# Issuing the value products of two attention units together, in a two-layer hybrid transformer kernel

## The chip, the cores and the metric

The kernel runs on one core of a Trainium2 chip. The metric is the device time of one execution in microseconds; the median over runs is compared. A core has a matrix engine (TensorE, PE in the profile, with its weight loads as PEld), a vector engine (DVE), an activation engine (ACT), GpSimd (POOL) and a queue that issues transfers (SP).

## The reference

Two transformer layers over 512 positions of 1024 channels, one batch. In each layer the input is normalised and modulated by vectors worked out from `c`, and one projection gives the inputs of three kinds of attention with heads of 64 channels: four heads that attend to selected keys (A), four stick-breaking heads (B), eight heads with a window of 128 and sinks (C). Their outputs are normalised per head, projected by `w_o` and added; a gated feed-forward of width 2816 follows.

```python
# A: a top-256 mask from an index score, softmax over the selected keys
_, sel = lax.top_k(score, n_sel)
p = jax.nn.softmax(s, axis=-1)
out = jnp.einsum('bhqk,bqkd->bqhd', p.astype(vs.dtype), vs)
# B: weights from a reversed cumulative sum of log_sigmoid
a = jnp.where(strict, jnp.exp(jax.nn.log_sigmoid(z) + log_between), 0.0)
out = jnp.einsum('bhqs,bshd->bqhd', a.astype(v.dtype), v)
# C: a band of 128 keys, one sink for each head
p = e / (jnp.sum(e, axis=-1, keepdims=True) + jnp.exp(sink - m))
out = jnp.einsum('bkgqs,bskd->bqkgd', p.astype(vn.dtype), vn)
```

The last line of each kind is the value product: weights times values.

## The kernel before

Positions are cut into four tiles of 128. Everything large is a matmul of three terms on split operands (a high and a low part each): projections, `w_o`, gate, up and down. The attention work is woven into this stream.

The order of PE's instructions is fixed while the program is built, by a planner, the class `Weaver` (L62). It keeps a clock `now` that advances by an assumed duration of each PE instruction (L277: a matmul with a tile position counts as `PVNS` = 80 ns), and a list of tasks written as generators. A task that yields a number is resumed when the clock has gone on by that many nanoseconds; one that yields a condition waits for it. The numbers come from two tables, `LAT` (L53) for layer 0 and `LAT2` (L54) for layer 1. They stand for the time that other engines need between two PE steps: `z` and `zp` from the stick-breaking scores to the cumulative product, `cum` from there to the value product, `C` and `A` from a unit's scores to its transposes, `pT` from the transposes to the value product, `fin` from the last product of an output bank to the transposes of the normalised output, `evac` until an output bank is free. The main stream of projection matmuls runs when no task is due. On the chip the engines run in that order and wait for each other by semaphores.

PSUM banks are few: three for scores (tag `z`), one for transposes (`t`), one for outputs (`o`, NO = 1 at L41). The output bank has one owner at a time (`own`, L120).

A value product is `pv` (L660): two matmuls, one for each half of 64 columns of the transposed weights, with a tile position; each half takes 64 of the array's columns. Three places use it.

- `pairB` (L1031): one generator for each pair of stick-breaking heads and layer; three groups of key blocks (3 and 2; 1; 0). In each group come the scores of both heads, softplus on ACT and DVE, the cumulative products, an exponential on ACT into a tile `at` for each head (four such buffers), and then, with a yield for each head (L1089 to L1100), the value products: 12 or 16 matmuls a head.
- `unitC` (L1200): four units for each tile of positions, two heads each. Two units share an output bank (`a["bank", t, hf]`, L1189). A unit makes its scores, the mask and maximum on DVE, the exponential on ACT, transposes into the `t` bank, a copy of it on ACT into a tile `pT` (two buffers, L1242), and after `pT` nanoseconds its value products: 8 matmuls in the first tile, 16 in the others. The second unit of a bank goes on to `finish_o` (L741), which copies and normalises.
- `unitA` (L1302): four units for each tile, one head each, all four in one output bank; 4, 8, 12 or 16 matmuls.

While C and A run, the main stream has the `w_o` products of the heads that are ready (L1376 to L1415).

Of the kernel before, what the change touches and what calls it, by code (L numbers as in the profile page):

```python
# [15 lines left out]
P = 128  # L16
L = 512
D = 1024
NT = L // P
# [30 lines left out]
MODRATE = 1.36  # L50
RESTN = 3
WB, WC, WA, WI = 1, 4, 4, 2
LAT = dict(sq00=1978, sq10=1972, sq01=1520, sq11=3460, rs00=2100, rs01=2833, rs10=1750, rs11=1150, zi=7704, ev=2194, oT2=2213, rope=18712, score=58, z=3680, cum=682, zp=830, C=2868, A=4170, pT=1011, fin=6768, oT=3509, cons=9020, kc=9275, mod=1094, sq=1869, rs=1526, u=2835, evac=699)  # L53
LAT2 = dict(zi=4392, ev=667, oT2=3700, rope=11698, score=286, z=2932, cum=702, zp=700, C=5010, A=848, pT=1144, fin=7203, oT=2208, cons=11900, kc=8549, evac=798)  # L54
PROXY = lambda e: e
LAB = ["?"]
EXPSET = "natural_log_exp_and_others"
# [157 lines left out]
def kernel(ctx, tc, x, c, lns, w_mod, b_mod, w_nat, w_qk, gains, sinks, g_out,  # L215
# [3 lines left out]
    wv = Weaver()  # L219
# [593 lines left out]
    def attention(l):  # L813
        lat = LATS[l]
# [216 lines left out]
        def pairB(pr):  # L1031

            qT, kT = a["qbT"][pr], a["kbT"][pr]
            acc = [None, None]
            key = ("B", l, pr)
            ob = None
            for grp in ((3, 2), (1,), (0,)):
                yield wv.take(["zz", "z"])
                yield "z"
                wv.give("zz")  # L1040
                a["Bz"] += grp == (0,)
                with lab("B"):
                    zbs = [bank("z") for _ in range(2)]
                    lay = []
                    o0 = 0
                    for j in grp:
                        w = (NT - j) * P
                        lay.append((j, o0, w))
                        o0 += w
                    for j, a0, w in lay:  # L1050
                        for i, zb in enumerate(zbs):
                            hp = slice(i * 64, i * 64 + 64)
                            T.matmul(zb[:, a0:a0 + w], kT[hp, j * P:(j + 1) * P], qT[hp, j * P:], start=(a0 == 0),
                                     stop=False, skip_group_check=True)
                    sps = []
                    for zb in zbs:
                        for j, a0, w in lay:
                            T.matmul(zb[:, a0:a0 + P], identb, bmaskb, start=False, stop=True, skip_group_check=True)
                        e = slot("e")
                        S.activation(e[:, :o0], zb[:, :o0], AF.Abs)  # L1060
                        act(e[:, :o0], e[:, :o0], AF.Exp, scale=-1.0)
                        act(e[:, :o0], e[:, :o0], AF.Ln, bias=1.0)
                        sp = slot("sp")
                        V.scalar_tensor_tensor(sp[:, :o0], zb[:, :o0], 0.0, e[:, :o0], op0=OP.max, op1=OP.add)
                        sps.append(sp)
                ats = []
                for i, (zb, sp) in enumerate(zip(zbs, sps)):
                    yield lat["zp" if i else "z"]
                    with lab("B"):
                        for j, a0, w in lay:  # L1070
                            T.matmul(zb[:, a0:a0 + w], ltri, sp[:, a0:a0 + w], start=False, stop=(j == NT - 1),
                                     skip_group_check=True)
                            if j == 2:
                                T.matmul(zb[:, a0 + P:a0 + w], nones, sp[:, :P], start=False, stop=True,
                                         skip_group_check=True)
                            elif acc[i] is not None:
                                T.matmul(zb[:, a0 + P:a0 + w], nones, acc[i], start=False, stop=True,
                                         skip_group_check=True)
                        at = slot("at")
                        act(at[:, :o0], zb[:, :o0], AF.Exp)  # L1080
                        ats.append(at)
                        if len(grp) == 2:
                            G.tensor_add(sp[:, 2 * P:3 * P], sp[:, 2 * P:3 * P], sp[:, :P])
                            acc[i] = sp[:, P:3 * P]
                        elif grp[0]:
                            G.tensor_add(sp[:, P:3 * P], sp[:, P:3 * P], acc[i])
                            acc[i] = sp[:, :3 * P]
                    wv.give("z", lat["cum"])
                for i, at in enumerate(ats):  # L1089
                    yield lat["cum"] if i else lat["cum"] / 2, wv.own(key)  # L1090
                    with lab("B"):
                        first = ob is None
                        if first:
                            ob = bank("o")
                        obv = ob.rearrange("p (t h d) -> p t h d", t=NT, h=2)
                        for j, a0, w in lay:
                            for t in range(j, NT):
                                pv(obv[:, t, i, :], at[:, a0 + (t - j) * P:a0 + (t - j + 1) * P],
                                   a["vb"][j][:, (2 * pr + i) * 64:(2 * pr + i + 1) * 64], first, j == 0)
                                first = False  # L1100
            with lab("B"):
                onB = slot("wk", (P, NT, 2, 64))
                finish_o(ob, 8, None, "ob", onB.rearrange("p t h d -> p (t h d)"))
            wv.later(lat["evac"], lambda: wv.owners.discard(key))
            wv.add(outB(pr, onB))
            a["B"] += 1
# [67 lines left out]
        def cons_qc(hf):  # L1174
            def cons(t, pb):
                with lab("C"):
                    v = rms_of(pb[:, :256], 4, "cv")
                    nat = slot("nat")
                    V.tensor_mul(hd(nat[:, :256], 4), hd(pb[:, :256], 4), bc(gn[:, l, 2], 4))
                    r = rsqrt(v, 4, "cr", EPS, G)  # L1180
                    G.tensor_scalar(a["rc"][:, t, 4 * hf:4 * hf + 4], r, 0.125, None, op0=OP.mult)
                    rope_apply(hd(nat[:, :256], 4), hd(nat[:, :256], 4), 4, t)
                    q = stacked(nat[:, :256], 4)
                yield lat["cons"], "w"
                with lab("C"):
                    a["qcT"][t][hf] = slot("hid")
                    heads_t(a["qcT"][t][hf], q, 4, lat)
                wv.give("nat", 200)
                a["bank", t, hf] = {"n": 0, "ob": None}  # L1189
                yield lat["ev"]  # L1190
                for i in range(2):
                    wv.add(unitC(t, 2 * hf + i), "C", WC)
            return cons
# [6 lines left out]
        def unitC(t, i):  # L1200
# [34 lines left out]
            with lab("C"):  # L1235
# [4 lines left out]
                                    p2[:, hh * 256 + j * P:hh * 256 + (j + 1) * P], ident)  # L1240
                pT = slot("pT")
                S.copy(pT[:, :2 * n], tb[:, :2 * n])  # L1242
            yield lat["pT"], lambda: a["B"] == 2
            wv.give("t")
            with lab("C"):
                if B["ob"] is None:
                    B["ob"] = bank("o")
                for hh in range(2):
                    for j in range(nb_):
                        pv(B["ob"][:, loc[hh] * 64:(loc[hh] + 1) * 64],  # L1250
                           pT[:, (hh * nb_ + j) * P:(hh * nb_ + j + 1) * P],
                           a["vc"][k0 // P + j][:, g * 64:(g + 1) * 64], j == 0, j == nb_ - 1)
                B["n"] += 1
                if B["n"] == 2:
                    es = small(4, "ces")
                    V.tensor_sub(es, B["nb"], nsk[:, l, 4 * g:4 * g + 4])
                    act(es, es, AF.Exp)
# [16 lines left out]
        def cons_a(t, pb):  # L1274
# [20 lines left out]
            wv.give("nat", 200)  # L1295
            yield lat["ev"]
            a["ka"] += 1
            a["A", t] = {"n": 0, "ob": None}
            for h in range(4):
                wv.add(unitA(t, h), "A", WA)  # L1300

        def unitA(t, h):  # L1302
# [22 lines left out]
            with lab("A"):  # L1325
# [2 lines left out]
                    T.transpose(tb[:, j * P:(j + 1) * P], p[:, j * P:(j + 1) * P], ident)  # L1328
                pT = slot("pT")
                S.copy(pT[:, :n], tb[:, :n])  # L1330
            yield (lat["pT"], wv.take(["on"])) if B["n"] == 3 else lat["pT"]
            wv.give("t")
            with lab("A"):
                if B["ob"] is None:
                    B["ob"] = bank("o")
                for j in range(t + 1):
                    pv(B["ob"][:, h * 64:(h + 1) * 64], pT[:, j * P:(j + 1) * P], a["va"][j], j == 0, j == t)
                B["n"] += 1
                if B["n"] == 4:
                    on = slot("on")  # L1340
                    finish_o(B["ob"][:, :256], 4, B["den"], "oa", on[:, :256])
                    wv.later(lat["evac"], lambda: wv.owners.discard(key))
                    wv.add(out_t(0, 2, on, t, "outA"))
# [271 lines left out]
```

## Time and profile before

| what | us |
|---|---|
| three runs, median (lowest, highest) | 1293.27 (1291.34, 1295.54) |
| profiled execution | 1292.21 |
| its span, first to last instruction | 1290.4 |
| PE busy | 1246.3 (97%) |
| DVE busy | 803.1 (62%) |
| ACT busy | 551.4 (43%) |
| POOL busy | 143.8 (11%) |

A busy time is the union of the engine's instruction rows. A matmul's row lasts from its start to the end of its results, so rows of one stream overlap; the distance from start to start tells what one costs. Layer 0's attention with value products runs from about 107 to 271 us of the span, layer 1's from about 741 to 894.

### The profile page before, as it was taken

The page shows a single profiled execution, that of the slowest core. Times are in us where ns is not written, and L with a number is a line of the kernel's source. Part 1 is how long each engine was busy: PE and PEld are TensorE (multiplying, and loading weights), DVE is VectorE, ACT ScalarE, POOL GpSimd, SP SyncE. Part 2 cuts the span into 40 slices and gives each one's busy share as a digit, 9 for nine tenths or more (in the row PEclk, how much of TensorE's full clock was granted, in tenths as well). Part 3 has the DMA queues.
Part 4 walks back from the last instruction along what each step waited for, and adds up shares of the span by engine and source line. Part 5 has one row for each costly group of instructions (what it writes and reads, how often), then busy time and mean ns, then how long its engine had stood idle before and what let it go on. Part 6 is the DMA issues. An engine that isn't in the chain of part 4 may idle for free.

```text
span 1290.4 us, 20282 instructions
## 1 busy us (share of the span) xinstructions
PE 1246.3 (97%) x7636; PEld 1045.4 (81%) x7636; DVE 803.1 (62%) x1805; ACT 551.4 (43%) x1211; POOL 143.8 (11%) x383
## 2 busy tenths in 40 slices
PE   5899999999999999999998999999999999999998
PEld 3687778689888888888887987977988888888887
DVE  4689877848467667644357999895655533433323
ACT  4445588746222222222245466885542222222220
POOL 0002333111000000000022034320300000000000
PEclk9999999999999999999999999999999999999999
DMA  9943131312468667533223211131145422322311
GB/s 338 336 158 104 63 118 35 107 50 76 142 192 252 188 223 245 153 122 98 75 82 98 66 34 34 35 116 49 43 135 159 139 78 86 127 61 92 112 50 66
DMA packets 60003, 152.77 MB, mean 118 GB/s; under 512 B 7296, under 2 KB 7808, under 8 KB 59904
## 3 DMA queue, kind: packets, MB, share of 16 engines
q1 hardware_dynamic: 59904, 151.47, 36.8%
q8 instruction: 60, 0.98, 0.3%
q14 instruction: 39, 0.32, 0.1%
HBM read 149.34 MB, written 2.10 MB: 117 GB/s over the span
## 4 chain that ended last, share of the span: by engine, by line
PE 79%; DVE 11%; ACT 5%; issue 2%; DMA 1%; POOL 1%; POOLq 0%; SPq 0%; DVEq 0%; ACTq 0%
PE z L280 39%; PE mm L280 33%; PE o L280 2%; PE t L283 2%; PE w L283 2%; DVE sp L290 2%; DVE wk L887 1%; PE t L280 1%; DVE top L886 1%; ACT p L319 1%; DVE nat L290 1%; DVE ws L592 1%; DVE rt L290 1%; PE w L280 1%; DVE actl L290 1%
## 5 line engine op out<-in xcount | busy, mean ns | idle before, releaser
L280 PE MATMUL z<-acth,ws 128*128 128x512 f32 x1312 | 408.4, 390 | 0.0
L592 DVE TENSOR_TENSOR ws<-raw,ws 128x1024 fp32r<-128x1024 f32 (+4 forms) x190 | 208.0, 1098 | 270.9 <-ACT ws L591 270.5
L591 ACT CAST ws<-raw 128x1024 fp32r<-128x1024 f32 (+4 forms) x190 | 178.9, 948 | 320.5 <-PE z L280 148.6
L280 PEld LDWEIGHTS z<-acth,ws 128*128 128x128 f32 x1312 | 246.3, 188 | 51.8 <-issue 0.8
L280 PE MATMUL mm<-hid,ws 128*128 128x512 f32 (+1 forms) x1212 | 272.2, 381 | 0.0
L280 PE MATMUL z<-actl,ws 128*128 128x512 f32 x656 | 255.4, 389 | 0.0
L280 PEld LDWEIGHTS mm<-hid,ws 128*128 128x128 f32 x1212 | 217.2, 188 | 40.4
L280 PE MATMUL mm<-ws,acth 128*128 128x256 f32 (+2 forms) x704 | 151.9, 309 | 0.0
L280 PEld LDWEIGHTS z<-actl,ws 128*128 128x128 f32 x656 | 123.2, 188 | 25.0
L280 PE MATMUL mm<-acth,ws 128*128 128x256 f32 (+1 forms) x544 | 128.3, 322 | 0.7 <-DVE xT L290 0.5
L280 PEld LDWEIGHTS mm<-ws,acth 128*128 128x128 f32 x704 | 111.8, 190 | 7.6 <-issue 3.8
L290 DVE SCALAR_TENSOR_TENSOR xT<-mm,mod,xT 128x512 f32<-128x512 f32 (+1 forms) x124 | 80.2, 660 | 58.4 <-PE mm L280 58.1
L280 PE MATMUL mm<-ws,actl 128*128 128x256 f32 (+2 forms) x352 | 103.7, 295 | 0.0
L280 PEld LDWEIGHTS mm<-acth,ws 128*128 128x128 f32 x544 | 91.3, 192 | 7.6 <-DVE xT L290 0.9
L319 ACT ACTIVATE e<-z 128x512 f32<-128x512 f32 x40 | 23.9, 597 | 160.9 <-PE z L280 160.9
L428 DVE SCALAR_TENSOR_TENSOR at<-nat,cs,at 128x512 f32<-128x512 f32 x98 | 73.2, 747 | 28.7 <-DMA nat<-in_w_mod_dram 27.9
L280 PE MATMUL mm<-actl,ws 128*128 128x256 f32 (+1 forms) x272 | 86.1, 316 | 0.0
L491 POOL TENSOR_TENSOR e<-e,on 128x256 f32<-128x256 f32 (+1 forms) x31 | 27.4, 883 | 399.1 <-ACT on L489 398.2
L280 PEld LDWEIGHTS mm<-ws,actl 128*128 128x128 f32 x352 | 66.7, 189 | 0.0
L280 PEld LDWEIGHTS mm<-actl,ws 128*128 128x128 f32 x272 | 52.2, 192 | 2.4
L886 DVE MAX8 top<-wk 128x8 f32<-128x384 f32 (+2 forms) x96 | 51.5, 552 | 0.6
L887 DVE MATCH_REPLACE8 wk<-top,wk 128x384 f32<-128x384 f32 (+2 forms) x96 | 51.8, 542 | 0.0
(230 smaller groups left out, 1520.8 us busy)
## 6 DMA issues: line engine op xcount, KB each, us to landing
raw<-in_w_gu_dram SPq DMA_DIRECT2D x88, 512.0 KB, 4.2
nat<-in_w_mod_dram SPq DMA_DIRECT2D x112, 256.0 KB, 3.4
raw<-in_w_dn_dram SPq DMA_DIRECT2D x48, 384.0 KB, 3.3
wk<-in_w_mod_dram SPq DMA_DIRECT2D x55, 256.0 KB, 5.4
raw<-in_w_nat_dram SPq DMA_DIRECT2D x16, 512.0 KB, 4.5
raw<-in_w_o_dram SPq DMA_DIRECT2D x16, 512.0 KB, 3.7
raw<-in_w_qk_dram SPq DMA_DIRECT2D x8, 512.0 KB, 4.9
raw<-in_w_mod_dram SPq DMA_DIRECT2D x8, 512.0 KB, 4.4
```

Source lines behind the costliest of these rows:

```text
L280: return self._done(T0.matmul(o, lhsT, rhs, **k), ns)
L283: return self._done(T0.transpose(o, i, idn), 109)
L290: ins = f(o, *a, **k)
L319: ins = S.activation(*a, **k)
L428: ins = V0.scalar_tensor_tensor(a, w, cs[:, k:k + 1], a, op0=OP.mult, op1=OP.add)
L491: self.eng.tensor_add(self.acc[:, sl], self.acc[:, sl], sq[:, sl])
L591: ops = [S.copy(sp[:, 0, :n], raw[:, :n])]
L592: ops.append(V0.tensor_sub(sp[:, 1, :n], raw[:, :n], sp[:, 0, :n].bitcast(F32)))
L886: pinned(V0.max(top8, sc[:, :n]), n)
L887: pinned(V0.match_replace(sc[:, :n], top8, sc[:, :n], TAKEN), n)
```

## The change

Value products are held back until two units of one output bank are ready, and are then issued in one loop. In C the first unit of a bank only leaves its `pT` tile in a list; the second issues the products of both. In A units one and two, and three and four, go together. In B the yield for each head becomes one yield, after which both heads' products are issued. Some of the planner's latencies in both tables are other numbers.

```diff
-LAT = dict(... oT2=2213, rope=18712, score=58, z=3680, cum=682, zp=830, C=2868, A=4170, pT=1011, fin=6768, ... sq=1869, rs=1526, u=2835, evac=699)
-LAT2 = dict(... score=286, z=2932, cum=702, zp=700, C=5010, A=848, pT=1144, fin=7203, oT=2208, cons=11900, kc=8549, evac=798)
+LAT = dict(... oT2=2031, rope=18712, score=70, z=5014, cum=786, zp=473, C=2312, A=3503, pT=1011, fin=7215, ... sq=1661, rs=1526, u=3327, evac=564)
+LAT2 = dict(... score=399, z=2932, cum=767, zp=700, C=5010, A=848, pT=879, fin=7479, oT=2208, cons=11900, kc=7631, evac=798)
...
-                for i, at in enumerate(ats):
-                    yield lat["cum"] if i else lat["cum"] / 2, wv.own(key)
-                    with lab("B"):
-                        first = ob is None
-                        if first:
-                            ob = bank("o")
-                        obv = ob.rearrange("p (t h d) -> p t h d", t=NT, h=2)
+                yield lat["cum"], wv.own(key)
+                with lab("B"):
+                    first = ob is None
+                    if first:
+                        ob = bank("o")
+                    obv = ob.rearrange("p (t h d) -> p t h d", t=NT, h=2)
+                    for i, at in enumerate(ats):
                         for j, a0, w in lay:
...
                 S.copy(pT[:, :2 * n], tb[:, :2 * n])
+                B["pv"].append((pT, loc))
+            B["n"] += 1
+            both = B["n"] == 2
             yield lat["pT"], lambda: a["B"] == 2
             wv.give("t")
+            if not both:
+                return
             with lab("C"):
...
-                for hh in range(2):
-                    for j in range(nb_):
-                        pv(B["ob"][:, loc[hh] * 64:(loc[hh] + 1) * 64],
-                           pT[:, (hh * nb_ + j) * P:(hh * nb_ + j + 1) * P],
-                           a["vc"][k0 // P + j][:, g * 64:(g + 1) * 64], j == 0, j == nb_ - 1)
-                B["n"] += 1
-                if B["n"] == 2:
+                for pT, loc in B["pv"]:
+                    for hh in range(2):
+                        for j in range(nb_):
+                            pv(B["ob"][:, loc[hh] * 64:(loc[hh] + 1) * 64],
+                               pT[:, (hh * nb_ + j) * P:(hh * nb_ + j + 1) * P],
+                               a["vc"][k0 // P + j][:, g * 64:(g + 1) * 64], j == 0, j == nb_ - 1)
+                if both:
...
                 S.copy(pT[:, :n], tb[:, :n])
-            yield (lat["pT"], wv.take(["on"])) if B["n"] == 3 else lat["pT"]
+                B["pv"].append((h, pT))
+            B["n"] += 1
+            seen = B["n"]
+            yield (lat["pT"], wv.take(["on"])) if seen == 4 else lat["pT"]
             wv.give("t")
+            if seen % 2:
+                return
             with lab("A"):
...
-                for j in range(t + 1):
-                    pv(B["ob"][:, h * 64:(h + 1) * 64], pT[:, j * P:(j + 1) * P], a["va"][j], j == 0, j == t)
-                B["n"] += 1
-                if B["n"] == 4:
+                for h, pT in B["pv"]:
+                    for j in range(t + 1):
+                        pv(B["ob"][:, h * 64:(h + 1) * 64], pT[:, j * P:(j + 1) * P], a["va"][j], j == 0, j == t)
+                B["pv"].clear()
+                if seen == 4:
```

## Rows read from the trace of the kernel before

**Rows 1.** Page, first part: busy time, share of the span, instructions.

```profile
PE 1246.3 (97%) x7636; PEld 1045.4 (81%) x7636; DVE 803.1 (62%) x1805; ACT 551.4 (43%) x1211; POOL 143.8 (11%) x383
```

**Rows 2.** Busy time by stretch: length, then each engine; then clock, DMA.

```profile
107.00:271.00 164.00, 155.74 (x1403) 125.43 (x1402) 134.04 (x432) 115.86 (x349) 50.27 (x164) 1.00 0.22 73
741.00:894.00 153.00, 146.17 (x1329) 121.62 (x1328) 130.88 (x420) 112.57 (x344) 52.33 (x162) 1.00 0.17 51
107.00:174.00 67.00, 62.65 (x537) 48.56 (x537) 60.09 (x171) 41.18 (x111) 25.07 (x73) 1.00 0.19 63
741.00:803.00 62.00, 59.20 (x515) 48.49 (x514) 59.44 (x168) 40.18 (x113) 28.71 (x78) 1.00 0.12 35
```

**Rows 3.** Timeline of PE around a stick-breaking burst: start, time, line, operation, count.

```profile
107.01 0.28 PE L280 MATMUL mm<-ws,actl 128*128 128x256 f32 x1
107.22 0.57 PE L280 MATMUL o<-wk,at 128*64 128x64 f32 x12
107.72 0.50 PE L280 MATMUL mm<-ws,acth 128*128 128x256 f32 x2
108.06 0.28 PE L280 MATMUL mm<-ws,actl 128*128 128x256 f32 x1
108.18 0.40 PE L280 MATMUL mm<-ws,acth 128*128 128x256 f32 x2
...
108.54 0.40 PE L280 MATMUL mm<-ws,acth 128*128 128x256 f32 x2
```

**Rows 4.** Timeline of PE around an A burst of four, and an undisturbed piece.

```profile
239.22 0.85 PE L280 MATMUL mm<-hid,ws 128*128 128x512 f32 x3
240.00 0.34 PE L280 MATMUL o<-va,pT 128*64 128x64 f32 x4
240.27 0.96 PE L280 MATMUL mm<-hid,ws 128*128 128x512 f32 x3
241.07 0.27 PE L283 MATMUL w<-cst,nat 128*128 128x128 f32 x1
...
271.20 0.63 PE L280 MATMUL mm<-acth,ws 128*128 128x512 f32 x2
271.67 0.39 PE L280 MATMUL mm<-actl,ws 128*128 128x512 f32 x1
271.90 0.63 PE L280 MATMUL mm<-acth,ws 128*128 128x512 f32 x2
```

**Rows 5.** Timeline of PE: transposes apart from a burst, and behind one.

```profile
175.95 0.38 PE L283 MATMUL t<-cst,p 128*128 128x128 f32 x2
...
177.45 0.45 PE L280 MATMUL o<-vc,pT 128*64 128x64 f32 x8
177.83 0.44 PE L283 MATMUL t<-cst,p 128*128 128x128 f32 x2
```

**Rows 6.** Output banks: duration ns least/median/most, first and last start.

```profile
L280 PE MATMUL o<-vc,pT x448: 221/222/272, 177.5 to 867.2; 128*64 128x64 f32 x150
...
L280 PE MATMUL o<-wk,at x320: 221/222/271, 107.2 to 802.7; 128*64 128x64 f32 x160
...
L280 PE MATMUL o<-va,pT x320: 221/222/271, 233.1 to 893.6; 128*64 128x64 f32 x160
```

**Rows 7.** Timeline of PE and ACT in layer 1's selected attention.

```profile
876.11 0.55 PE L283 MATMUL t<-cst,p 128*128 128x128 f32 x3
...
876.96 0.47 ACT L1330 COPY pT<-t 128x384 f32<-128x384 f32 x1
...
877.49 0.57 PE L280 MATMUL o<-va,pT 128*64 128x64 f32 x12
```

**Rows 8.** Waits of PE's weight loads, whole run: us in total, times, longest.

```profile
PEld z L280 <- DVE sp L290: 7.0, 6, 2.2
...
PEld o L280 <- ACT pT L1330: 6.9, 13, 1.5
...
PEld o L280 <- ACT pT L1242: 4.3, 10, 0.8
```

**Rows 9.** Chain of work that ended last: start, time, what.

```profile
270.70 5.76 PE mm L280 x30
```

More of the change, by code (lines that the diff above doesn't have):

```diff
@@ L52 @@
 WB, WC, WA, WI = 1, 4, 4, 2
-LAT = dict(sq00=1978, sq10=1972, sq01=1520, sq11=3460, rs00=2100, rs01=2833, rs10=1750, rs11=1150, zi=7704, ev=2194, oT2=2213, rope=18712, score=58, z=3680, cum=682, zp=830, C=2868, A=4170, pT=1011, fin=6768, oT=3509, cons=9020, kc=9275, mod=1094, sq=1869, rs=1526, u=2835, evac=699)
-LAT2 = dict(zi=4392, ev=667, oT2=3700, rope=11698, score=286, z=2932, cum=702, zp=700, C=5010, A=848, pT=1144, fin=7203, oT=2208, cons=11900, kc=8549, evac=798)
+LAT = dict(sq00=1978, sq10=1972, sq01=1520, sq11=3460, rs00=2100, rs01=2833, rs10=1750, rs11=1150, zi=7704, ev=2194, oT2=2031, rope=18712, score=70, z=5014, cum=786, zp=473, C=2312, A=3503, pT=1011, fin=7215, oT=3509, cons=9020, kc=9275, mod=1094, sq=1661, rs=1526, u=3327, evac=564)
+LAT2 = dict(zi=4392, ev=667, oT2=3700, rope=11698, score=399, z=2932, cum=767, zp=700, C=5010, A=848, pT=879, fin=7479, oT=2208, cons=11900, kc=7631, evac=798)
 PROXY = lambda e: e
@@ L1188, in cons @@
                 wv.give("nat", 200)
-                a["bank", t, hf] = {"n": 0, "ob": None}
+                a["bank", t, hf] = {"n": 0, "ob": None, "pv": []}
                 yield lat["ev"]
@@ L1297, in cons_a @@
             a["ka"] += 1
-            a["A", t] = {"n": 0, "ob": None}
+            a["A", t] = {"n": 0, "ob": None, "pv": []}
             for h in range(4):
```

## The prediction

> **What bounds the kernel now.** I read the page's first part, then the busy time of the attention stretches, then TensorE's instructions one by one. The page gives PE 1246.3 us busy of a span of 1290.4 [rows 1]: a change pays mainly by what it takes out of PE's own stream. In the two stretches in which value products run, PE idles 164 - 155.74 = 8.3 us in layer 0 and 153 - 146.17 = 6.8 us in layer 1 [rows 2]; the granted clock is 1.00, its 2.4 GHz level, throughout them. No other engine is full over a whole stretch, but in the stick-breaking part of layer 1 DVE is busy 59.44 of 62 us against PE's 59.20 [rows 2]: there DVE sets the pace, and less PE work need not shorten it.
>
> Busy time does not tell what a value product costs, since its row lasts 222 ns while a pair starts every few dozen ns. I read starts. Undisturbed, 256-wide matmuls come three in 0.36 us (108.18 to 108.54), 0.12 each [rows 3]. Around a burst of 12 value products, from 107.01 to 108.18, 1.17 us pass with four such matmuls in them (0.48), so the burst took 0.69. Undisturbed 512-wide matmuls come three in 0.70 us (271.20 to 271.90), 0.233 each [rows 4]. Around a burst of 4, from 239.22 to 241.07, 1.85 us pass with six of them (1.40): 0.45. Eight more products (four pairs) cost 0.24, or 0.06 a pair, and what is left at zero pairs is 0.45 - 2 x 0.06 = 0.33 (from the 12: 0.69 - 0.36 = 0.33). So a burst has a **fixed price of 0.33 us**, whatever its size: a gap before it, a slow first pair, a gap behind it, and a slow first matmul after it. Where transposes follow, the last part is smaller: two transposes are drawn out from 0.38 to 0.44 us behind a burst [rows 5], two matmuls from 0.40 to 0.50 [rows 3], so there 0.04 comes off: 0.29.
>
> The Trainium skill (TensorEngine Tiling (Array Packing), Key Properties) says that changing the tiling mode, not just the tile, drains the engine. The same page (Performance Considerations, Instruction Overhead) gives about 60 cycles of overhead to every matmul, which alone would make 12 products cost three times 4, and regrouping worth nothing. By the first rule the regrouping would save about what I take; by the second its sum would be 0. The trace has 0.69 against 0.45 us, a ratio of 1.5 and not 3, so it sides with the first.
>
> **The change part by part.**
>
> *Bursts removed.* The rows count 320 stick-breaking, 448 window and 320 selected value products [rows 6]. By the loops these are 2 layers x 2 pairs x 3 groups x 2 heads = 24 bursts, 2 x 4 tiles x 4 units = 32, and 2 x 4 x 4 = 32: 88. After the change two consecutive ones stand together: 44. The products themselves are unchanged. Removed: 12 stick-breaking bursts at 0.33 = 4.0 us, and 32 of the other two kinds at 0.29, since the next unit's transposes usually follow them = 9.3 us. Gross gain 13.3 us.
>
> *What of it is not kept.* In the stick-breaking part of layer 1 DVE paces; I count its six bursts (6 x 0.33 = 2.0) as lost to waiting for DVE. In the selected-attention part of layer 1 there is a stretch where PE has nothing but transposes, scores and value products: transposes at 876.11, the copy on ACT at 876.96 for 0.47, value products at 877.49 [rows 7]. PE waits there for that copy. The burst itself is in that chain, so its price shrinks the chain too, but a wait for exponentials may take the place; I count half of its eight bursts as lost (8 x 0.29 / 2 = 1.2). In all 3.2. From both ends: nothing is lost (0), or all that lies in the two layer-1 parts and as much in layer 0 (2 x (2.0 + 2.3) = 8.6). I take 3.2 because layer 0 leaves DVE more room, 60.09 of 67 us [rows 2], and there the idle rows are nearer to zero.
>
> *Waits moved.* The first unit's products no longer wait for its copy, but the second unit's transposes follow that copy anyway: they write the one transpose bank, which the copy must have left. So the wait moves from the value product to the transpose and costs what it did. Both copies now live until the joint burst; there are two such buffers, and the third copy's transposes stand behind the burst on PE, so its ACT copy waits for nothing new. In the stick-breaking groups the first head's products now stand behind the second head's exponential, as the second's already did; four buffers of that kind cover two heads and the next group. On ACT, POOL and SP's queue nothing is added or passed. The joint burst is longer by 8 pairs at most (0.5 us), which delays the final copy of an output bank only by work that had to come before it anyway. All this I take at 0.
>
> *The two tables of times.* Besides, the planner's latencies change: in layer 0 z goes up by 1.33 us, zp down by 0.36, C and A down by 0.56 and 0.67, fin up by 0.45; in layer 1 pT down by 0.27, fin up by 0.28, kc down. They alter only when an instruction is put into PE's order, not its work. At best they remove idle time: all of it is 8.3 + 6.8 = 15.1 us [rows 2], of which the stick-breaking products' wait for DVE's softplus, the one that a longer z addresses, is 7.0 us in the weight-load rows of the whole run [rows 8]. At worst they add: a longer z makes a layer-0 group longer, per group 1.33 - 0.36, less 0.24 that the joint yield saves (0.34 + 0.68 before, 0.79 after), 0.73, and for six groups 4.4 us, by which attention ends later with the same filler. That filler is 5.76 us of matmuls behind the last burst [rows 9], and it covers most of the last unit's normalisation; 4.4 of it could turn into idle time. I take 0, near the middle, and keep -7 and +4.4 for the range.
>
> **Sum.** -13.3 + 3.2 = -10.1 us. Against the profiled execution (1292.21 us, span 1290.4 and 1.8 around it) that is 1282.1; that execution is 1.06 below the median of the runs, and from the median 1293.27 the forecast is **1283 us**.
>
> **Rivals.**
>
> 1. *The gain is bigger*: nothing is lost to other engines and the longer z removes about half of the softplus wait: -13.3 - 3.5, 1276.5. For it: PE is 97% busy, so most stretches keep what is saved. Against: DVE in layer 1. Chance 0.15.
> 2. *The gain is mostly hidden*: PE waits for copies, exponentials and DVE in both layers, the 8.6 us above are lost, and little else is won: -13.3 + 8.6 = -4.7, 1288.6, up to 1293 if the tail of layer 0 also loses its cover. For it: PE waited for ACT's transposed copies in 13 + 10 = 23 of 64 units already [rows 8]. Against: elsewhere projection matmuls stand between the units. Chance 0.14, nearly half of it faster by over 0.3%.
> 3. *Slower*: the place is the ACT copy between a unit's transposes and what follows on PE. With the first burst gone from between, and in layer 1 with pT 0.27 shorter, each copy is looked for too early. A wait now costs (6.9 + 4.3) / 23 = 0.49 us [rows 8]; if all the other 41 units wait as long, 41 x 0.49 = 20.0 us come in, and the time is 1293.3 - 13.3 + 20.0 = 1300. It decides from 27 new waits (13.3 / 0.49) for no gain, and from 35 for slower by 0.3%. For it: in the starved stretch every unit waits. Against: that is a dozen units, and in the rest other matmuls of the planner stand between. Chance 0.13, of which 0.05 end within 0.3%.
> 4. *The change doesn't do what it says*: the planner puts other work between the two units' products, or the price is per product and not per burst: 1293. The rows of 4 and 12 products speak against the second, the code (one uninterrupted loop) against the first. Chance 0.04.
>
> My own case has 0.54, with a range of 1279 to 1287. A measurement of this kernel can tell some 0.3%, 3.9 us, from no change. Faster by more (below 1289.4): 0.54 + 0.15 + 0.06 = 0.75. Within: 0.08 + 0.05 + 0.04 = 0.17. Slower: 0.08. The range 1277 to 1294 leaves out about half of rival 1 and most of rival 3, some 0.18.
>
> **What would show it.** Value products in runs of 8 to 32 and 44 runs in the PE timeline; the same count of products; about 0.3 us of price per run; PE's busy time in the two stretches lower by about as much as the time; DVE's share of the layer-1 stick-breaking part near 100%. The weight-load waits for the two copies should keep their sum near 11 us while some pass to the transposes. The prediction is wrong if these waits double, if idle time appears behind the last burst of layer 0, or if the stretches keep their lengths of 164 and 153 us.

## The result, and the profile after

The changed kernel takes 1286.22 us (median of six runs, 1282.25 to 1290.43), the kernel before in the same comparison 1294.87. The ratio is 0.9937, with an interval of 0.9918 to 0.9957: about 8 us faster, where 10 were forecast. The profiled execution took 1283.93 us with a span of 1282.1. The page's first part, against [rows 1]:

```profile
PE 1236.7 (96%) x7636; PEld 1042.9 (81%) x7636; DVE 800.3 (62%) x1805; ACT 549.8 (43%) x1211; POOL 142.8 (11%) x383
```

The count of instructions is the same. PE's busy time fell by 9.6 us and the span by 8.3, so 1.3 us came back as idle time. The count of value products is also that of [rows 6]:

```profile
L280 PE MATMUL o<-vc,pT x448: 222/222/271, 175.9 to 847.9; 128*64 128x64 f32 x150
...
L280 PE MATMUL o<-wk,at x320: 222/222/271, 107.9 to 795.1; 128*64 128x64 f32 x160
...
L280 PE MATMUL o<-va,pT x320: 222/222/271, 227.3 to 885.3; 128*64 128x64 f32 x160
```

They stand in 44 runs now. The timeline of PE around one of 32, the counterpart of [rows 4]:

```profile
262.85 0.40 PE L280 MATMUL mm<-acth,ws 128*128 128x512 f32 x1
263.18 1.15 PE L280 MATMUL o<-va,pT 128*64 128x64 f32 x32
264.26 0.50 PE L280 MATMUL mm<-acth,ws 128*128 128x512 f32 x1
264.60 0.39 PE L280 MATMUL mm<-actl,ws 128*128 128x512 f32 x1
264.83 0.62 PE L280 MATMUL mm<-acth,ws 128*128 128x512 f32 x2
```

From 262.85 to 264.83 pass 1.98 us with three 512-wide matmuls (0.70) in them, so 32 products took 1.28: 16 pairs at 0.058 are 0.93, and 0.35 is left. (A pair starts 0.058 us after the one before it, 6 or 7 ns from half to half and 51 or 52 to the next pair.) The fixed price is that of a burst of 4 or 12; it is only paid half as often. Taken the same way over all bursts that a matmul follows and no wait stands at, the median is 0.35 us at 4 products and 0.34 at 12 in the kernel before, and 0.35 at 32 in the changed one.

The waits of PE's weight loads, against [rows 8] (us in total, times, longest):

```profile
PEld t L283 <- ACT pT L1242: 4.2, 6, 1.1
PEld z L280 <- DVE sp L290: 3.9, 4, 1.7
...
PEld o L280 <- ACT pT L1335: 1.4, 3, 0.9
...
PEld t L283 <- ACT pT L1335: 1.2, 3, 0.5
...
PEld o L280 <- ACT pT L1242: 0.9, 2, 0.6
```

L1335 is the line of A's copy in the changed kernel, L1330 in the kernel before. Of the wait for the two transposed copies 5.4 us stand at the transposes now and 2.3 at the value products, 7.7 together where it was 11.2; the wait for softplus fell from 7.0 to 3.9.

**A balance of PE's starts.** To compare whole kernels I cut the same two pieces of work out of each, from the 500th to the 2600th matmul and from the 4300th to the 6400th (the attention of each layer and a little beside it; the transposes that e3 and e4 add are not counted, but lie inside the pieces), and took from every distance between starts the undisturbed distance of that form. What is left over was put down to the bursts where it lies ahead of, inside or behind one, or on the first matmul after it, unless it is over 0.2 us; all else is "rest": waits, a lower clock, and steps between forms that are the same in all kernels. A price that hides behind a wait is counted as rest, 17 times at some 0.09 us in the kernel before, 7 times in the changed one. In us, from one profiled execution each, with the ratio of the timed runs to the kernel before:

| kernel | layer 0 | layer 1 | bursts | their price | rest | ratio (95%) |
|---|---|---|---|---|---|---|
| before | 275.3 | 278.9 | 88 | 25.3 | 36.5 | 1 |
| changed | 271.6 | 275.4 | 44 | 13.9 | 41.1 | 0.9937 (0.9918, 0.9957) |
| e1, new tables alone | 280.6 | 284.6 | 88 | 25.5 | 47.8 | 1.0075 (1.0061, 1.0089) |
| e2, joining, old tables | 277.5 | 281.4 | 44 | 13.9 | 52.9 | 1.0035 (1.0023, 1.0047) |
| e3, a matmul between units | 273.4 | 281.9 | 76 | 22.5 | 37.4 | 0.9997 (0.9986, 1.0007) |
| e4, the same ahead of a burst | 270.2 | 277.3 | 44 | 13.7 | 38.4 | 0.9950 (0.9937, 0.9963) |
| e5, joining, new z, zp, cum; pT | 273.4 | 281.9 | 44 | 14.3 | 49.1 | 1.0010 (0.9995, 1.0026) |
| e6, joining, the other entries new | 280.3 | 277.4 | 44 | 14.0 | 48.5 | 1.0010 (0.9999, 1.0021) |
| e7, C and A joined alone | 272.5 | 276.5 | 56 | 17.6 | 39.4 | 0.9938 (0.9922, 0.9953) |
| e8, B joined alone | 274.6 | 280.3 | 76 | 21.7 | 41.3 | 1.0004 (0.9993, 1.0016) |
| e9, joining, old tables, 42 ns | 284.2 | 284.0 | 44 | 14.1 | 62.3 | 1.0106 (1.0090, 1.0121) |
| e10, changed, 42 ns | 270.8 | 283.4 | 44 | 13.4 | 48.9 | 0.9990 (0.9981, 1.0000) |
| e11, before, 52 ns | 277.4 | 284.5 | 88 | 25.4 | 44.6 | 1.0045 (1.0031, 1.0059) |
| e12, changed, tables a tenth back | 271.4 | 277.3 | 44 | 14.1 | 42.7 | 0.9955 (0.9939, 0.9972) |

In the changed kernel the bursts' price is 11.4 us lower and the rest 4.6 higher. The price comes out alike in all kernels with 44 bursts (13.4 to 14.3). The rest depends on the execution: the profiled execution of e1, e3 and e11 took 2.4 to 3.4 us more than the median of its runs, that of the changed kernel and of e4 2.3 and 3.0 less. So a rest is good to some 3 us only.

### The profile page after: what moved, and what is told of

It reads as the page before. It is cut to its first block, busy times and chain, and to the rows that moved or that the text cites. A ratio compares the mean times of both kernels' runs of the same rounds, so it can differ in the third digit from the quotient of the medians.

```text
span 1282.1 us, 20284 instructions
## 1 busy us (share of the span) xinstructions
PE 1236.7 (96%) x7636; PEld 1042.9 (81%) x7636; DVE 800.3 (62%) x1805; ACT 549.8 (43%) x1211; POOL 142.8 (11%) x383
## 4 chain that ended last, share of the span: by engine, by line
PE 79%; DVE 12%; ACT 4%; issue 2%; POOL 1%; DMA 1%; SPq 0%; POOLq 0%; DVEq 0%; ACTq 0%
PE z L280 39%; PE mm L280 33%; PE o L280 2%; DVE sp L290 2%; PE t L283 1%; DVE wk L887 1%; PE w L283 1%; DVE top L886 1%; ACT p L319 1%; DVE nat L290 1%; DVE ws L592 1%; DVE actl L290 1%; DVE rt L290 1%; PE t L280 1%; PE w L280 1%
## 5 line engine op out<-in xcount | busy, mean ns | idle before, releaser
L428 DVE SCALAR_TENSOR_TENSOR at<-nat,cs,at 128x512 f32<-128x512 f32 x98 | 73.2, 747 | 27.0 <-DMA nat<-in_w_mod_dram 26.2
```

The source lines that it names most:

```text
L428: ins = V0.scalar_tensor_tensor(a, w, cs[:, k:k + 1], a, op0=OP.mult, op1=OP.add)
```

## The experiments

The theory at the start: a burst has a price, 44 of them went, and some of it was paid back in waits. The rival: the new latencies made the kernel faster and the joining only came along. The first two runs take the change apart.

**e1**: the kernel before with the new tables, and nothing joined.

```diff
-LAT = dict(... z=3680, cum=682, zp=830, C=2868, A=4170, ... fin=6768 ...)
+LAT = dict(... z=5014, cum=786, zp=473, C=2312, A=3503, ... fin=7215 ...)   # LAT2 likewise
```

> The kernel before with only the two tables of planner latencies of the changed kernel; value products stay in 88 bursts. Price theory (each burst costs 0.29 to 0.33 us and the joining takes 44 of them away): the bursts' own cost stays near 25 us in the PE starts, and the time stays within 4 us of the kernel before (1291 to 1299). Table theory (the retimed steps are what made it faster): 8 us faster than before, near 1287.

1302.16 us against 1292.03: slower by 10, which neither theory had. The bursts' price stayed (25.5). What came in shows in PE's own waits (us in total, times, longest), in layer 0's attention and the start of the feed-forward:

```profile
PE o L280 <- ACT pT L1330: 3.2, 3, 1.8
PE o L280 <- ACT pT L1242: 2.2, 3, 1.2
PE w L283 <- DVE on L290: 2.0, 1, 2.0
```

and in layer 1's:

```profile
PE o L280 <- ACT pT L1242: 3.5, 5, 0.9
PE o L280 <- ACT pT L1330: 3.2, 5, 0.9
PE z L280 <- DVE sp L290: 2.8, 3, 1.8
```

Value products wait 12.1 us for their copies, where they waited 4.5 in the whole run before. I read it so: with C and A shorter in layer 0 and pT in layer 1, a unit is driven on too early for a kernel that needs its copy at once. No run changes these entries by themselves. The `on` row is the wait for the last unit's normalisation behind layer 0's last burst.

**e2**: the joining with the old tables.

```diff
-LAT = dict(... z=5014, cum=786, zp=473, C=2312, A=3503, ... fin=7215 ...)
+LAT = dict(... z=3680, cum=682, zp=830, C=2868, A=4170, ... fin=6768 ...)   # LAT2 likewise
```

> The changed kernel with the two tables of the kernel before. Price theory: 44 bursts, their own cost down by 11 to 13 us, the time faster than before by most of what the changed kernel gained, 5 to 12 us. Table theory: no faster than the kernel before (within 2 us), since the joining is paid back in waits. Third possibility: tables and joining need each other, then both this run and the one with the tables alone are slower than the changed kernel by 4 us or more.

1297.81 us, slower than the kernel before by some 4.5. The price fell as in the changed kernel, to 13.9, and the rest rose by 16.4. The third possibility holds: joining and tables need each other. The wait of PE's weight loads that stands out most against the changed kernel is the one for softplus, 10.4 us where it has 3.9:

```profile
PEld z L280 <- DVE sp L290: 10.4, 8, 3.2
...
PEld t L283 <- ACT pT L1335: 3.8, 5, 1.1
...
PEld t L283 <- ACT pT L1242: 3.6, 5, 1.3
```

PE's own idle time in the two pieces is 16.1 us in the kernel before, 26.2 here and 18.2 in the changed kernel. Of the 8.0 us between the last two, 5.7 are the wait for softplus (8.7 and 3.0; before 5.2).

**e3 and e4** measure the price by itself. Both add the same 32 transposes to the changed kernel and take them out of the planner's clock (the last line of the diff). PE's order of all other instructions is then that of the changed kernel, in both.

```diff
-                for pT, loc in B["pv"]:
+                for u, (pT, loc) in enumerate(B["pv"]):
+                    if u == 1:              # e3; in e4: u == 0. The same in unitA
+                        T.transpose(B["ob"][:, 256:384], ident, ident)
+                        wv.now -= 109
```

> The changed kernel with one more transpose of the identity into an unused part of the output bank, between the two units' value products of every joint burst of C and A (32 of them; the planner's clock leaves them out, so that the rest of PE's order stays). Price theory: against the same matmul ahead of the burst it is slower by 32 x 0.30 = 9 to 10 us; in the PE starts 32 more bursts with the price of 0.30 each. If the price were per product, or lay in cover that other engines give, the two would be equal within 2 us.

> The control: the changed kernel with the same 32 extra transposes of the identity, each ahead of its joint burst. Price theory: 32 x 0.11 = 3.5 us slower than the changed kernel, or less where PE would wait anyway; still 44 bursts. Per-product theory: the same 3.5 us, and equal to the run with the matmul between.

1291.8 against 1286.47 us: splitting 32 bursts costs 5.3 us by the medians (by the two ratios 6, give or take 2), and the transposes alone, ahead of the burst, cost nothing that can be measured. A split burst in the timeline of PE, in e3:

```profile
208.33 0.45 PE L280 MATMUL o<-vc,pT 128*64 128x64 f32 x8
208.72 0.33 PE L283 MATMUL o<-cst 128*128 128x128 f32 x1
208.97 0.45 PE L280 MATMUL o<-vc,pT 128*64 128x64 f32 x8
209.36 0.74 PE L280 MATMUL z<-hid,hid 128*128 128x256 f32 x4
```

and the same burst in e4:

```profile
205.80 0.27 PE L283 MATMUL o<-cst 128*128 128x128 f32 x1
206.00 0.69 PE L280 MATMUL o<-vc,pT 128*64 128x64 f32 x16
206.62 0.74 PE L280 MATMUL z<-hid,hid 128*128 128x256 f32 x4
```

From the first row to the scores pass 1.03 us in the one and 0.82 in the other, 0.21 more, with the slow transpose that follows a burst included. Over the two attentions the bursts' price is 22.5 - 13.7 = 8.8 us higher, 0.27 a split, of which 5 to 6 show in the timed runs. Per product and not per burst, both would have taken the same: that rival is out. The Trainium skill says that a change of tiling mode drains TensorE (TensorEngine Tiling (Array Packing), Key Properties); these runs agree in that each time in and out has its price, 0.27 us; the drain itself no row shows.

**e5 and e6** divide the tables: the entries of the stick-breaking steps in layer 0 and pT in layer 1, or all the others.

```diff
-LAT = dict(... z=5014, cum=786, zp=473, C=2312, A=3503 ...);  LAT2 = dict(... pT=879, fin=7479, kc=7631 ...)
+LAT = dict(... z=5014, cum=786, zp=473, C=2868, A=4170 ...);  LAT2 = dict(... pT=879, fin=7203, kc=8549 ...)   # e5
+LAT = dict(... z=3680, cum=682, zp=830, C=2312, A=3503 ...);  LAT2 = dict(... pT=1144, fin=7479, kc=7631 ...)  # e6
```

> The changed kernel with the tables of the kernel before, but in layer 0 the new z, zp and cum, in layer 1 the new pT. Attention took 277.5 and 281.4 us in the two layers with the joining and all old tables, 271.6 and 275.4 in the changed kernel. If the stick-breaking latencies carry layer 0 and pT carries layer 1: 272 and 276, and the time within 2 us of the changed kernel. If other entries (C, A, fin, kc) carry it: 277 and 281, some 4 us slower than the kernel before. A split (one layer as the changed kernel, one as the other) says which entry matters where.

> The complement: the changed kernel with its tables, but in layer 0 the old z, zp and cum, in layer 1 the old pT. If those four entries carry the gain: 277 and 281 us and some 4 us slower than the kernel before. If the others carry it: 272 and 276 and as fast as the changed kernel. If every entry matters only together with the rest, both this run and its complement lie between.

1294.31 and 1294.07 us, both as the kernel before. The lengths of the two pieces, from one execution each, split: z, zp and cum bring layer 0 from 277.5 to 273.4, most of the way to 271.6, and without them it takes 280.3; in layer 1 pT alone gives nothing (281.9), while score, cum, fin and kc without it give 277.4.

**e7 and e8** divide the joining, both with the new tables.

```diff
-                yield lat["cum"], wv.own(key)
+                for i, at in enumerate(ats):          # e7: B as before, C and A joined; e8: the reverse
+                    yield lat["cum"] if i else lat["cum"] / 2, wv.own(key)
```

> The changed kernel (joining and new tables), but the stick-breaking heads are issued one by one as before: 56 bursts. Price theory: against the changed kernel 12 bursts x 0.33 = 4 us more in the bursts' own cost, and up to 4 us slower; less where DVE sets the pace. If the joining of the heads cost waits of its own, it is as fast as the changed kernel or faster.

> The kernel before with the new tables and only the stick-breaking heads joined: 76 bursts. With the new tables and no joining at all TensorE waited 12.1 us for the transposed copies ahead of value products and the time was 10 us above the kernel before. If the joining in C and A is what takes these waits away, they stay near 12 us here and the time is 5 to 10 us above the kernel before. If the tables and the heads' joining are enough, it is as fast as the kernel before.

e7 takes 1285.48 us and has the ratio of the changed kernel. Joining the stick-breaking heads on top of it saves 3.7 us of price; the two pieces together are 2.0 us shorter (549.0 and 547.0), and the timed runs, which tell some 3 us here, show no difference. e8 is as fast as the kernel before, and its value products wait 8.2 us for copies, fewer than e1's 12.1 and yet nearly twice the 4.5 of before. Against e1 the same joining of heads is worth 9 us by the ratios (1.0075 to 1.0004), of which only 3.8 are price: what a joining is worth in waits depends on what else is in the kernel.

**e9, e10 and e11** test a theory of why joining adds waits. The planner books 80 ns for a product; by the starts it costs 42 when joined and 52 before. So a joint burst of 32 is booked at 2.56 us and takes 1.26, and what is resumed behind it would come 1.3 us too early.

```diff
-PVNS = 80
+PVNS = 42          # e9 with the old tables, e10 the changed kernel; e11: 52 in the kernel before
```

> The changed kernel with the old tables, and the planner books 42 ns for a value product in place of 80 (by the starts in the trace a product costs (13.9 + 1088 x 0.029) / 1088 = 0.042 us when joined, 0.052 before). Theory of the over-booked burst: a joint burst of 32 is booked at 2.56 us and takes 1.26, so what is resumed behind it comes 1.3 us too early, where a burst of 16 was only 0.5 us off; booked right, the waits in attention fall from 52.9 us towards the 36.5 of the kernel before, and the time from 4 us above that kernel to 5 us or more below it. Rival (the joining itself holds work back, or the old latencies were fitted to the old order by chance): the waits stay above 48 us and the time no faster than the kernel before.

> The changed kernel, new tables, booked at 42 ns. Theory of the over-booked burst: its waits (41.1 us) fall by a few us, as fast as the changed kernel or faster by up to 4 us. Rival (the new tables are fitted to the 80 ns, so any other order costs): slower than the changed kernel by 4 us or more, waits above 46 us.

> The control without joining: the kernel before with 52 ns booked for a value product. Over-booked burst: some of its waits (36.5 us) go, faster by 0 to 4 us. Rival (tables fitted to one order): slower by 3 us or more, as the tables alone were slower by 10.

All three are slower than with 80: 1306.87, 1292.36 and 1299.27 us. The rest went up, from 52.9 to 62.3, 41.1 to 48.9 and 36.5 to 44.6. In the form tested the theory falls: a truer booking alone made none of the three kernels faster. The tables stayed those of the kernels that book 80 ns, and none for 42 was tried.

**e12**: what the runs up to here suggested was that any new order loses. So the changed kernel's tables were moved a tenth of the way back.

```diff
-LAT = dict(... z=5014, cum=786, zp=473, C=2312, A=3503 ...)
+LAT = dict(... z=4881, cum=776, zp=509, C=2368, A=3570 ...)   # LAT2 likewise
```

> The changed kernel with each changed table entry moved a tenth of the way back to its old value (layer 0: z 5014 to 4881, C 2312 to 2368, A 3503 to 3570 and so on). If the new tables are better estimates of real latencies, a tenth hardly matters: within 2 us of the changed kernel, waits in attention of 40 to 43 us. If they are fitted to one order of instructions, a tenth already gives another order and most of the gain goes: slower than the changed kernel by 3 us or more, waits above 45 us, with the bursts' own cost still near 14.

1286.75 us, a ratio of 0.9955 to the kernel before, its interval overlapping that of the changed kernel, though PE's order differs from it in 373 of 7636 places. So the gain doesn't hang on one order of instructions; the rough sizes of the entries are enough. No version beat the changed kernel by more than can be measured.

## Why the prediction was right, and which of its steps were not

*The fixed price of a burst, 0.33 and 0.29 us, and 13.3 us gross.* Right in kind: e3 against e4 shows it with everything else held. In size it is 11.4 us by the balance: 7.7 for the 32 bursts of C and A, where I had 9.3 (e7 against the kernel before), and 3.7 for the 12 of B, where I had 4.0. Some 0.9 comes on top if the 17 and 7 times count that it hid behind a wait.

*Not kept: 3.2 us.* In sum close: the rest rose by 4.6. But it isn't shown to come from where I put it. I had the whole 2.0 us of layer 1's stick-breaking lost because DVE paces there, and nothing in layer 0's. From e7 to the changed kernel the piece of layer 1 shortens by 1.1 us and that of layer 0 by 0.9, each of some 1.9 of price: layer 1 kept no less. And DVE was no fixed pace. Busy time in layer 1's stick-breaking part (length, then PE, PEld, DVE, ACT, POOL), against the last of [rows 2]:

```profile
737.00:794.50 57.50, 53.23 (x469) 43.72 (x468) 54.87 (x149) 38.05 (x102) 23.62 (x70) 1.00 0.13 38
```

DVE's share is 95%, as before, but the part has fewer DVE instructions (149, where there were 168) and fewer matmuls (469, where there were 515), and is shorter: from its first value product to its last 57.6 us, where it was 60.8. Other work of both engines stands elsewhere now, so the length of the part doesn't say what was kept of the price.

*Waits moved, taken at 0.* This step failed. That the wait for the first copy passes to the second unit's transposes is seen (5.4 of 7.7 us). For the copies the sum even holds with the old tables (10.3 us in e2, 2.9 at the value products and 7.4 at the transposes, against the 11.2 of [rows 8]). But that the joining adds no wait is wrong: with the old tables the rest rises by 16.4 us, more than the price that goes, and the kernel is slower than before. I followed each buffer and each queue for a new dependence and found none. What I left out is that a later product shifts everything behind it in PE's one order, and old latencies can then place a step where its input is not ready. The rows show it for softplus, whose wait in the weight loads went from 7.0 us [rows 8] to 10.4; for the rest of the 16.4 it is argued.

*The two tables, taken at 0 and bounded by -7 and +4.4.* This failed too, and outside its bounds: with the joining they take 11.8 us off the rest (52.9 to 41.1), without it they add 11.3 (36.5 to 47.8). One term cannot be right for them, since their worth depends on the joining. The two mistakes cancel to +4.6. That they did so is luck, as far as the prediction goes: the forecast of 1283 us lies close to the 1286.22 measured because 16.4 and -11.8, both taken at 0, nearly make up for each other, and not because either was known.

*The rivals.* The place of rival 3, the ACT copies between transposes and what follows, is where e1 lost most of its time (12.1 us of waits at value products, where it was 4.5); with the joining the second unit's work stands between. Rival 4's price per product is excluded by e3 and e4. Idle time behind layer 0's last burst, which I feared from the longer z, appeared in e1 (2.0 us for `on`), not in the changed kernel.

*What stays open.* Which wait in the joined kernel with old tables is the first, from which others follow, is not settled. Softplus is the largest that I can name (10.4 us against 3.9), and z, zp and cum do mend layer 0; for layer 1 I have no single entry, and the theory of the over-booked burst did not help.

## What to carry to other kernels

In this kernel small tiled matmuls were dear by the number of times the engine goes into and out of their mode: compare bursts of two sizes, start to start, and the zero point of the line is the price. Where a planner with a table of latencies writes the order, a change of structure and its table are one change: time each alone and both before crediting either, and price a table by the waits of the kernel that it goes with. A balance of PE's starts into price and rest tells the two apart where the total hides them.

## What was not expected of the hardware

A wait of PE can cost more than its length. Here a wait for ACT of 1.94 us, in layer 0 of the changed kernel, in the timeline of PE:

```profile
220.44 0.27 PE L283 MATMUL t<-cst,p 128*128 128x128 f32 x1
222.65 1.06 PE L280 MATMUL mm<-hid,ws 128*128 128x512 f32 x3 [1.94 <-ACT ary L319]
223.52 0.52 PE L280 MATMUL z<-hid,ws 128*128 128x128 f32 x2
223.84 1.59 PE L280 MATMUL mm<-hid,ws 128*128 128x512 f32 x3
225.22 0.41 PE L283 MATMUL t<-cst,p 128*128 128x128 f32 x1
```

and the busy time of the stretches after it, with the granted clock in the third column from the right:

```profile
223.30:226.70 3.40, 3.40 (x11) 2.63 (x10) 2.89 (x10) 1.02 (x4) 1.77 (x6) 0.50 0.64 249
226.70:230.00 3.30, 3.30 (x28) 2.84 (x27) 2.54 (x10) 1.34 (x6) 0.37 (x1) 1.00 0.02 5
```

The granted clock stands at 0.50, the 1.2 GHz level, after the engine had stood. Three 512-wide matmuls take 1.38 us there (223.84 to 225.22), where they took 0.70 in [rows 4]; then the clock is back at 1.00. At half the clock this stretch loses an estimated 1.7 us (half of its 3.4), nearly as much as the wait itself. The Trainium skill has the same two levels and lays the lower one to an idle engine (TensorE: Matmul & The Clock Gate, What's actually happening). The trace agrees in the levels, at 0.50 and 1.00, and in the order, the wait ahead of the fall.

But not every wait of this length brings the clock down. The kernel before has one of 1.99 us in layer 0, with 1.00 over the whole stretch [rows 2], and e2 one of 3.02 us that no lower clock follows:

```profile
167.47 1.12 PE L280 MATMUL z<-sp,cst 128*128 128x512 f32 x2 [1.99 <-DVE sp L290]
...
165.10 1.13 PE L280 MATMUL z<-sp,cst 128*128 128x512 f32 x2 [3.02 <-DVE sp L290]
```

What decides it, these runs don't show. Stretches at 0.50 stand in the attention of most of the slower kernels (e9 has five; the kernel before, e4 and e8 have none), and one each in the changed kernel, e7 and e12. So part of what is "rest" above is not waiting but slow matmuls behind a wait. By the undisturbed distances of the matmuls that start in such stretches I estimate 1.7 us of it in the changed kernel, 2.9 in e2, 3.3 in e1 and 7.1 in e9: the smaller part of the differences in rest. The clock also shows in the spread of the timed runs: of the six of the changed kernel the one with a mean clock of 0.997 has a span of 1280.4 us, the one with 0.989 of 1288.6.
